# Writing TensorE's order by hand in the attention stage of a hybrid decoder layer

## The chip, the cores and the metric

The kernel runs on one core of a Trainium2 chip. The metric is the device time of one execution in microseconds (us), as the median of several runs. TensorE (PE in the profile) does the matrix products, ScalarE (ACT) the activations and copies, VectorE (DVE) and GpSimd (POOL) elementwise work, and SyncE (SP) issues most of the loads.

## The reference, cut to what matters

One decoder layer on 1024 tokens of width 1024, in float32. The first half mixes tokens: the normalised input is projected once, and the columns of the projection go to two groups of heads. One is attention over a sliding window of 128 with 8 query heads, 2 key-value heads, a learned sink per head and a partial rotation of queries and keys. The other is a gated linear recurrence with 4 heads of 128. Both are normalised, joined and projected. The second half is a dense MLP with squared ReLU.

```python
h = rmsnorm(x, pre_w_mix[l]) * (1.0 + sc1) + sh1
proj = h @ w_in[l]
aq, ak, av, hq, hf, hi, hg = jnp.split(proj, _SPLITS, axis=-1)
aq = partial_rope(aq.reshape(B, T, ATT_Q_HEADS, ATT_HEAD_DIM))
ak = partial_rope(ak.reshape(B, T, ATT_KV_HEADS, ATT_HEAD_DIM))
attn = sliding_window_sink_attention(aq, ak, av, attn_sinks[l])   # softmax over two 128-blocks, with sink
attn = rmsnorm(attn, attn_out_w[l])
...
rec = hgrn2_chunkwise(hq4, 1.0 - f, hv4, jnp.log(f))              # hv4 comes from hi
mix = jnp.concatenate([attn, rec], axis=-1) @ w_out[l]
x = x + g1 * rmsnorm(mix, post_w_mix[l])
```

## The kernel before, in words

Tokens are handled in eight blocks of 128 (`tb` from 0 to 7, `TB` = 8), and the width of 1024 in eight blocks of 128 (`kb`, `KB` = 8). A float32 operand of a projection is split into a high and a low part, and a projection is made of three products a `kb`: high by high, high by low, low by high (`proj3`, line 517). A projection of one token block is thus 24 products into one PSUM bank: of 512 columns for the queries (tile `pq`, weights `wq`) and for the recurrence's values (`pv`, weights `whv`), and of 256 columns for keys and values (`pk`, weights `wkv`).

The kernel is written with a framework that traces instructions, sets the semaphores and gives out the buffers of its pools. A scheduler in it sets the order of each engine's instructions ahead of time, by readiness in its own model and by the place in the text. A small class `Queue` (line 28) stands before each engine. While an engine is pinned (`pin(True, ...)`), each instruction is chained behind the one issued before it, so the engine runs them in the order of the text. Once it is unpinned, instructions are only held behind the last pinned one, and the scheduler orders them. Up to line 689 all compute engines are pinned; line 690 unpins them.

The queries of blocks 0 to 5 and the keys and values of blocks 0 to 3 are projected before that line. What is left for the attention stage is: the keys and values of blocks 4 to 7, the queries of blocks 6 and 7, and the recurrence's values of all eight blocks. They serve as filler between the steps of attention.

The generator `attention(tb)` (line 577) holds one block's attention. By the names of the tiles:

- `pqT`, `pkT`: the queries and keys are transposed on PE and copied (`qT` by ACT, `kT` by DVE).
- `sc`: the scores against this block and the one before, in two halves (`mp`). ACT copies the older block's part into `comb` and DVE copies this block's part under the mask `mle`.
- DVE takes the maximum (`mx`), ACT the exponentials, DVE and POOL divide by the sum.
- `pT`: the weights are transposed on PE; DVE parts them into this block's (`pc`) and the older block's (`pp`).
- `oT`: the output; ACT squares it (`sqa`), DVE multiplies it by `attw` and sums the squares (`sqr`).
- `ssp`: the sums are transposed on PE, DVE reduces them (`ssc`), POOL makes the reciprocal root (`t_att`, `r_att`), DVE puts it on a diagonal (`dg`).
- `rb`: a product spreads it, and DVE multiplies the output by it. The result stays in the tile of the queries.

Before the change the generator has three parts, cut behind the division, behind `dg`, and at the end. The loop at line 723 runs `i` from 0 to 15: at each `i` it takes the parts of the blocks that are due by `att_a` and then one filler, a whole projection of 24 products. With the eighth filler the weights `whv` are loaded and split (`load_split`, line 244: a load by SP, a high part by ACT, a low part by DVE). They take the slots of the pool `g_` that `wq` and others held. At `i` of 12, 13 and 15 a piece of the adaLN modulation begins (`mods`; `modrow` at line 168, `modcols` at line 157): eight loads of 256 KB on SP and the sum `macc` on DVE; for the first two also a broadcast on POOL's queue and a split. PSUM has two banks for projections (`mm_ps`), five for attention (`tp_ps`) and one (`pa`) that `ssp` and `rb` share.

After the stage come the four heads of the recurrence, whose first projection is `phf`, with weights `whf0`.

Of the kernel before, what the change touches and what calls it, by code (L numbers as in the profile page):

```python
# [19 lines left out]
TB = 8  # L20
# [27 lines left out]
def hybrid_layer(ctx: ExitStack, tc: tile.TileContext, I, out, dbg=None):  # L48
# [3 lines left out]
    def pin(on, *engines):  # L52
        for e in engines:
            e.pinned = on
# [478 lines left out]
    cosT = cload("cosT", [P, TB, 16], pool=XA)  # L533
    sinT = cload("sinT", [P, TB, 16], pool=XA)

    def qproj(tb):
        if tb < 6:
            pq = pq0[tb]
        else:
            pq = mm_ps(f"pq{tb}")  # L540
            proj3(pq, htok(tb), wq)
        q = m_(f"q{tb}")
        ACT.activation(q, pq, AF.Copy, scale=0.125)
        qn.append(q)

    def kvproj(tb):
        if tb < 4:
            pk = pk0[tb]
        else:
            pk = mm_ps(f"pk{tb}")  # L550
            proj3(pk[:, :256], htok(tb), wkv)
# [25 lines left out]
    def attention(tb):  # L577
# [8 lines left out]
        kT = XA.tile([P, P], F32, tag="kT", bufs=3, name=f"kT{tb}")  # L586
        DVE.tensor_copy(kT, pkT[:, :P])
        kTs[tb] = kT
        aw = q
        a3 = aw.rearrange("p (m t) -> p m t", m=4)  # L590
        c5 = w_(f"comb{tb}", (P, 2, 2, 2, P))
# [4 lines left out]
        for mp in range(2):  # L596
            scs = [tp_ps(f"sc{tb}_{mp}_{g}").rearrange("p (m j) -> p m j", m=2) for g in range(2)]
            for m in range(2):
                for src in (tb - 1, tb) if tb else (tb,):
                    for g in range(2):  # L600
                        gs = slice(64 * g, 64 * g + 64)
                        js = slice(P, 2 * P) if src == tb else slice(0, P)
                        PE.matmul(scs[g][:, m, js], lhsT=qT[gs, 2 * mp + m, :], rhs=kTs[src][gs, :],
                                  start=True, stop=True)
            for g in range(2):
                sc = scs[g]
                if tb:
                    ACT.activation(c5[:, mp, g], sc[:, :, 0:P], AF.Copy)
                DVE.copy_predicated(c5[:, mp, g], mb, sc[:, :, P:2 * P])
        mx = small.tile([P, 8], F32, tag="mx", name=f"mx{tb}")  # L610
        DVE.tensor_reduce(mx, c, AX.X, ALU.max)
        mx2 = small.tile([P, 8], F32, tag="mx2", name=f"mx2{tb}")
# [57 lines left out]
    def step(tb):  # L670
        if 0 <= tb < TB:
            next(att[tb])

    att = [attention(tb) for tb in range(TB)]
    pq0.append(a_ps("pq4"))
# [16 lines left out]
    def filler(i):  # L692
        if i < 8:
            (kvproj if i % 2 else qproj)(4 + i // 2)
            rope(4 + i // 2, 2 if i % 2 else 8)
        else:
            values(i - 8)


    whv = []  # L700
    hv = []

    def values(tb):
        if not tb:
            for kb in range(KB):
                whv.append(load_split(g_, f"whv{kb}", I["w_hv"][kb]))
        pv = mm_ps(f"pv{tb}")
        proj3(pv, htok(tb), whv)
        v = hv_(f"hv{tb}")
        ACT.activation(v, pv, AF.Copy)  # L710
        hv.append(v)

    a2 = tiny1.tile([P, KB], F32, tag="a2", name="a2")
    sh2 = tiny1.tile([P, KB], F32, tag="sh2", name="sh2")
# [1088 lines left out]
```

## Time and profile before

| what | value |
|---|---|
| median of 3 runs | 1085.75 us (1085.65 to 1085.79) |
| the profiled execution's own time | 1085.71 us |
| its span, first to last instruction | 1083.8 us |
| TensorE's granted clock, mean | 0.998 |
| TensorE busy | 1068.5 us of the span |
| VectorE busy | 806.9 us |
| ScalarE busy | 589.1 us |
| GpSimd busy | 373.8 us |
| DMA traffic | 205.74 MB |

Busy time counts an engine's instructions without what its sequencer does. Matmuls overlap in their pipeline and their ends are modelled, so the spacing of their starts says more than their lengths. A bracket behind a row of a timeline gives the engine's idle time just before that row and what ended it. Nearly all instructions carry line 39, which is the `Queue` class's call, so the rows are told apart by their tiles.

### The profile page before, as it was taken

To read this page: it belongs to the slowest core of one execution; us is meant where nothing else is said; L and a number is where in the kernel's file an instruction comes from. 1 tells how busy PE (TensorE), PEld (TensorE's weight loads), DVE (VectorE), ACT (ScalarE), POOL (GpSimd) and SP (SyncE) were. 2 spreads that over 40 slices of the span, in tenths; PEclk is the share of its full clock that TensorE was granted. 3 is DMA by queue.
4 is the path that set the end of the run, shared out by engine and by line. 5 is a ranking of instruction groups with operands and counts; after the bars stand their busy time and mean duration, and the time that the engine had idled before them with its cause. 6 is when DMAs were issued, how large, how long until landed. Compare 5 with 4: busy or idle time off the path is not lost.

```text
span 1083.8 us, 16059 instructions
## 1 busy us (share of the span) xinstructions
PE 1068.5 (99%) x5449; PEld 872.3 (80%) x5449; DVE 806.9 (74%) x1329; ACT 589.1 (54%) x1215; POOL 373.8 (34%) x497
## 2 busy tenths in 40 slices
PE   8999999999999999999999999999999999999996
PEld 6887676788888888888888888888888888888885
DVE  4877778878765664558777767776767787899886
ACT  4556453546456655576655555555764544456434
POOL 1263211233325653423443434444333333230014
PEclk9999999999999999999999999999999999999999
DMA  9904002444211242323676777767998888998638
GB/s 358 345 21 130 27 1 82 156 148 137 75 59 55 95 173 94 130 89 126 214 250 216 252 233 231 258 219 259 326 355 295 276 292 265 313 325 285 192 95 141
DMA packets 102979, 205.74 MB, mean 190 GB/s; under 512 B 13168, under 2 KB 13936, under 8 KB 102896
## 3 DMA queue, kind: packets, MB, share of 16 engines
q1 hardware_dynamic: 87408, 157.14, 42.7%
q0 software_dynamic: 15200, 47.20, 14.8%
q8 instruction: 43, 0.70, 0.3%
q10 hardware_dynamic: 288, 0.36, 0.1%
q14 instruction: 40, 0.33, 0.1%
HBM read 149.60 MB, written 55.05 MB: 189 GB/s over the span
## 4 chain that ended last, share of the span: by engine, by line
PE 90%; DVE 4%; DMA 3%; ACT 1%; issue 1%; POOL 1%; DVEq 0%; SPq 0%; ACTq 0%; POOLq 0%
PE pda L39 16%; PE pua L39 14%; PE pdc L39 8%; PE po L39 8%; PE puc L39 7%; PE pu L39 4%; PE pdb L39 4%; PE phg L39 4%; PE phq L39 4%; PE pub L39 4%; PE phf L39 3%; PE pv L39 3%; PE pq L39 3%; DMA wa<-wada 1%; PE o L39 1%; DVE macc L39 1%
## 5 line engine op out<-in xcount | busy, mean ns | idle before, releaser
L39 POOL TENSOR_TENSOR b<-b,b 128x512 f32<-128x512 f32 x64 | 90.1, 1407 | 235.8 <-DMA b<-w_dn 235.5
L39 ACT ACTIVATE s<-s 128x512 f32<-128x512 f32 x84 | 52.9, 631 | 32.8 <-DVE s L39 31.5
L39 ACT ACTIVATE dw<-dwr 128x512 fp32r<-128x512 f32 x72 | 45.4, 631 | 41.4 <-DMA dwr<-td 24.7
L39 DVE TENSOR_TENSOR acc<-pda,acc 128x512 f32<-128x512 f32 x68 | 46.5, 684 | 15.0 <-PE pda L39 14.6
L39 DVE TENSOR_TENSOR dw<-dwr,dw 128x512 fp32r<-128x512 f32 x72 | 53.2, 739 | 5.6 <-ACT dw L39 5.6
L39 POOL DMA_DIRECT2D td<-b x64 | 36.3, 567 | 19.0 <-POOL b L39 19.0
L39 ACT ACTIVATE s<-pua 128x512 f32<-128x512 f32 x28 | 16.7, 596 | 40.0 <-PE pua L39 34.5
L39 DVE TENSOR_TENSOR wt<-s,wt 128x512 fp32r<-128x512 f32 x42 | 35.5, 846 | 2.6 <-ACT wt L39 2.5
L39 ACT ACT_TABLE_LOAD x28 | 35.9, 1283 | 1.7 <-PEq L1796 1.2
L39 POOL TENSOR_TENSOR rrf<-ssf,mhalf 128x1 f32<-128x1 f32 x7 | 7.8, 1107 | 83.3 <-DVE ssf L39 83.3
L39 DVE SCALAR_TENSOR_TENSOR macc<-wada,cs,macc 128x512 f32<-128x512 f32 x42 | 33.7, 803 | 2.2 <-DMA wada<-wada 1.7
L39 POOL DMA_DIRECT2D b<-w_dn x64 | 34.4, 540 | 2.5 <-issue 2.5
L39 PE MATMUL pua<-bt_0h,wt 128*128 128x512 f32 x84 | 32.7, 389 | 0.0
L39 PE MATMUL pua<-bt_1h,wt 128*128 128x512 f32 x84 | 32.7, 389 | 0.0
L39 PE MATMUL pua<-bt_2h,wt 128*128 128x512 f32 x84 | 32.7, 389 | 0.0
L39 PE MATMUL pua<-bt_3h,wt 128*128 128x512 f32 x84 | 32.7, 389 | 0.0
L39 DVE TENSOR_TENSOR wt<-a,wt 128x512 fp32r<-128x512 f32 x42 | 31.8, 758 | 0.9 <-ACT wt L39 0.9
L39 POOL TENSOR_TENSOR comb<-comb,rd 128x512 f32<-128x512 f32 x8 | 11.7, 1457 | 59.9 <-DVE rd L39 44.2
L39 ACT ACTIVATE wt<-s 128x512 fp32r<-128x512 f32 x42 | 26.3, 627 | 8.4 <-DVE s L39 8.2
L39 DVE TENSOR_TENSOR acc<-pdc,acc 128x512 f32<-128x512 f32 x36 | 24.6, 684 | 7.2 <-PE pdc L39 7.1
L39 PE MATMUL pdc<-dw,du_3h 128*128 128x512 f32 x96 | 29.6, 389 | 0.0
L39 PE MATMUL pda<-dw,du_7h 128*128 128x512 f32 x96 | 29.6, 389 | 0.0
(768 smaller groups left out, 3748.7 us busy)
## 6 DMA issues: line engine op xcount, KB each, us to landing
dur<-ud SPq DMA_DIRECT2D x112, 256.0 KB, 4.9
wada<-wada SPq DMA_DIRECT2D x64, 256.0 KB, 3.5
b<-w_dn POOLq DMA_DIRECT2D x64, 256.0 KB, 5.5
td<-b POOLq DMA_DIRECT2D x64, 256.0 KB, 3.4
dwr<-td SPq DMA_DIRECT2D x64, 256.0 KB, 4.6
a<-w_u SPq DMA_DIRECT2D x56, 256.0 KB, 4.2
dwr<-w_dn SPq DMA_DIRECT2D x48, 256.0 KB, 4.8
ud<-s SPq DMA_DIRECT2D x42, 256.0 KB, 3.6
```

Source lines behind the costliest of these rows:

```text
L39: ins = op(*args, **kw)
```

## The change

The generator `attention` is cut into seven parts in place of three: behind the copies of `qT` and `kT`, between the halves of the scores, behind the division as before, behind `pc` and `pp`, behind `sqr`, behind `dg` as before, and at the end.

The projections become closures for single products in a list `feed_q`. `feed(us)` takes products from its front until their stated times (0.227 us for 512 columns, 0.12 us for 256) add up to `us`. The last product of a projection also issues its copy and its rotation. PE stays pinned, so that it runs products and steps as written, until the turn t = 6 of the loop; ACT, DVE and POOL are unpinned as before. The loads of `whv` and their splits stand earlier in the text, ahead of the last queries' products. The first two pieces of the modulation begin at t = 6 and 7, the third behind the loop.

```diff
+    feed_q = []
+    def feed(us):
+        while us > 0 and feed_q:
+            fn, w = feed_q.pop(0)
+            fn()
+            us -= w
+    def queue3(pst, lhs, rhs, us, done):
+        n = len(lhs)
+        for k in range(n):
+            for i in range(3):
+                def fn(k=k, i=i):
+                    (ah, al), (bh, bl) = lhs[k], rhs[k]
+                    PE.matmul(pst(), lhsT=al if i == 2 else ah, rhs=bl if i == 1 else bh,
+                              start=(k == 0 and i == 0), stop=(k == n - 1 and i == 2))
+                    if k == n - 1 and i == 2:
+                        done()
+                feed_q.append((fn, us))
...
         kTs[tb] = kT
+        yield
...
                 DVE.copy_predicated(c5[:, mp, g], mb, sc[:, :, P:2 * P])
+            if not mp:
+                yield
...
                 DVE.tensor_tensor(pp[:, mp], pT3, pc[:, mp], ALU.subtract)
+        yield
         o_ps = tp_ps(f"oT{tb}")
...
         DVE.tensor_reduce(sqr, sq.rearrange("p (m t) -> p t m", m=4), AX.X, ALU.add)
+        yield
         ssp = pa.tile([P, 512], F32, tag="aps", name=f"ssp{tb}")
...
-    pin(False, ACT, DVE, POOL, PE)
+    pin(False, ACT, DVE, POOL)
...
+    def values(tb):
+        pv = bank(f"pv{tb}")
+        def done():
+            v = hv_(f"hv{tb}")
+            ACT.activation(v, pv(), AF.Copy)
+            hv.append(v)
+        queue3(pv, htok(tb), whv, 0.227, done)
...
-    att_a = (4, 5, 6, 7, 8, 9, 10, 11)
-    mod_a = (12, 13, 15)
-    for i in range(16):
-        for tb in range(TB):
-            if i in (att_a[tb], att_a[tb] + 2, att_a[tb] + 3):
-                step(tb)
-        filler(i)
-        if i in mod_a:
-            next(mods[mod_a.index(i)])
+    for tb in (4, 5):
+        qproj(tb)
+        rope(tb, 8)
+    for tb in (4, 5):
+        kv_later(tb)
+    for tb in (6, 7):
+        q_later(tb)
+        kv_later(tb)
+    def step(tb):
+        if tb < TB:
+            next(att[tb], None)
+    feed(4.4)
+    step(0)
+    feed(0.9)
+    step(0)
+    step(0)
+    for kb in range(KB):
+        whv.append(load_split(g_, f"whv{kb}", I["w_hv"][kb]))
+    for tb in range(TB):
+        values(tb)
+    feed(4.8)
+    step(1)
+    feed(1.9)
+    step(1)
+    step(1)
+    feed(1.2)
+    step(0)
+    feed(2.6)
+    for t in range(TB):
+        if t > 5:
+            next(mods[t - 6])
+        step(t)
+        step(t + 2)
+        feed(2.6 if t < 6 else 2.8)
+        step(t + 2)
+        step(t)
+        step(t + 2)
+        feed(1.0 if t < 6 else 2.2)
+        if t == 6:
+            pin(False, PE)
+        step(t)
+        step(t + 1)
+        if t < 6:
+            feed(3.3)
+        else:
+            feed(99)
+    next(mods[2])
     gactx.close()
```

`bank(name)` gives a projection its PSUM bank when its first product is issued. `kv_later` and `q_later` are made like `values`, with the copy and the rotation in their last call.

More of the change, by code (lines that the diff above doesn't have):

```diff
@@ L534, in hybrid_layer, with bank, pst @@
     sinT = cload("sinT", [P, TB, 16], pool=XA)
-    def qproj(tb):
[L537 to L541, printed above, removed]
+    feed_q = []
[15 more added lines that the diff above has]
+                feed_q.append((fn, us))
+    def bank(name):
+        got = []
+        def pst():
+            if not got:
+                got.append(mm_ps(name))
+            return got[0]
+        return pst
+    def qproj(tb):
+        pq = pq0[tb]
         q = m_(f"q{tb}")
@@ L546, in kvproj @@
     def kvproj(tb):
[L547 to L551, printed above, removed]
+        pk = pk0[tb]
         kv = XA.tile([P, 256], F32, tag="kv", bufs=8, name=f"kv{tb}")
@@ L668, in attention @@
         yield
-    def step(tb):
-        if 0 <= tb < TB:
-            next(att[tb])
     att = [attention(tb) for tb in range(TB)]
@@ L689, in hybrid_layer, with kv_later, q_later, done @@
         rope(tb, 2, eng)
-    pin(False, ACT, DVE, POOL, PE)
[L692 to L697, printed above, removed]
+    pin(False, ACT, DVE, POOL)
     whv = []
     hv = []
-    def values(tb):
[L704 to L711, printed above, removed]
+    def kv_later(tb):
+        pk = bank(f"pk{tb}")
+        def done():
+            pk0.append(pk())
+            kvproj(tb)
+            rope(tb, 2)
+        queue3(lambda: pk()[:, :256], htok(tb), wkv, 0.12, done)
+    def q_later(tb):
+        pq = bank(f"pq{tb}")
+        def done():
+            pq0.append(pq())
+            qproj(tb)
+            rope(tb, 8)
+        queue3(pq, htok(tb), wq, 0.227, done)
+    def values(tb):
+        pv = bank(f"pv{tb}")
+        def done():
+            v = hv_(f"hv{tb}")
+            ACT.activation(v, pv(), AF.Copy)
+            hv.append(v)
+        queue3(pv, htok(tb), whv, 0.227, done)
     a2 = tiny1.tile([P, KB], F32, tag="a2", name="a2")
@@ L720, in hybrid_layer @@
         mods += [modcols(3, half, m_, sh2), modcols(4, half, m_, sc2)]
-    att_a = (4, 5, 6, 7, 8, 9, 10, 11)
-    mod_a = (12, 13, 15)
-    for i in range(16):
-        for tb in range(TB):
-            if i in (att_a[tb], att_a[tb] + 2, att_a[tb] + 3):
-                step(tb)
-        filler(i)
-        if i in mod_a:
-            next(mods[mod_a.index(i)])
+    for tb in (4, 5):
+        qproj(tb)
+        rope(tb, 8)
+    for tb in (4, 5):
[42 more added lines that the diff above has]
+    next(mods[2])
     gactx.close()
```

## The prediction

> **What bounds the kernel now.** I read the page first (busy shares, then the chain that ended last), then the busy times by windows of 24 us over the attention stage, then TensorE's own timeline from 74 to 192 us, and last the timelines of VectorE (DVE) and GpSimd (POOL) for the same stretch.
>
> ```profile
> PE 1068.5 (99%) x5449; PEld 872.3 (80%) x5449; DVE 806.9 (74%) x1329; ACT 589.1 (54%) x1215; POOL 373.8 (34%) x497
> ...
> PE 90%; DVE 4%; DMA 3%; ACT 1%; issue 1%; POOL 1%; DVEq 0%; SPq 0%; ACTq 0%; POOLq 0%
> ```
>
> TensorE (PE) is busy throughout and carries 90% of the chain: a microsecond of PE time lost in the stage is a microsecond of the kernel, and so is one saved. The change adds and removes no matmul, so all it can win is time in which PE waits, or issues more slowly than it could.
>
> ```profile
> 122.00:146.00 24.00, 23.98 (x158) 16.99 (x156) 17.23 (x42) 12.27 (x48) 3.46 (x6) 1.00 0.00 1
> ...
> 170.00:194.00 24.00, 22.57 (x101) 16.16 (x100) 21.54 (x37) 7.10 (x12) 4.27 (x6) 1.00 0.43 134
> ```
>
> The columns are length, then busy time of PE, weight load, DVE, ACT and POOL, the granted clock, and DMA. In the middle of the stage PE has no gap and the clock is full; at its end DVE is the fuller engine (21.54 of 24 us). One period of the middle, from PE's timeline (start, length, instructions):
>
> ```profile
> 130.67 1.09 PE L39 MATMUL oT<-pp,kv 128*64 128x512 f32 x4
> ...
> 132.55 0.66 PE L39 MATMUL pqT<-c_tab,q 128*128 128x128 f32 x4
> 133.04 0.27 PE L39 MATMUL pkT<-c_tab,kv 128*128 128x128 f32 x1
> 133.07 0.48 PE L39 MATMUL pv<-whv4h,hhi 128*128 128x512 f32 x1
> ...
> 133.95 0.71 PE L39 MATMUL sc<-kT,qT 64*128 64x128 f32 x8
> 134.59 0.51 PE L39 MATMUL pv<-whv5h,hhi 128*128 128x512 f32 x1
> 135.11 0.33 PE L39 MATMUL ssp<-c_tab,sqr 128*128 128x128 f32 x1
> 135.19 0.47 PE L39 MATMUL pv<-whv5l,hhi 128*128 128x512 f32 x1
> 135.60 1.61 PE L39 MATMUL sc<-kT,qT 64*128 64x128 f32 x24
> 137.13 0.49 PE L39 MATMUL rb<-dg,ones 128*128 128x128 f32 x2
> 137.46 1.04 PE L39 MATMUL pT<-c_tab,comb 128*128 128x128 f32 x8
> 138.25 0.49 PE L39 MATMUL pv<-whv5h,hlo 128*128 128x512 f32 x1
> ...
> 143.25 1.08 PE L39 MATMUL oT<-pp,kv 128*64 128x512 f32 x4
> ```
>
> Start to start, three products take 133.95-133.07 = 0.88 us and 21 products 143.25-138.25 = 5.00. So a product costs (5.00-0.88)/18 = 0.229 us, and each unbroken group of products 0.19 us more, for entering and leaving the attention's fp32 work. The two groups of one product cost 0.52 and 0.41, or 0.29 and 0.18 over the product. The period is 12.58 us with 3+1+1+21 = 26 products: 5.95 us for products, 6.63 for everything else. Ahead of and behind this steady part PE does wait (the bracket is the idle time and what ended it):
>
> ```profile
> 94.87 0.94 PE L39 MATMUL sc<-kT,qT 64*128 64x128 f32 x12
> ...
> 97.39 0.49 PE L39 MATMUL pq<-wq7h,hlo 128*128 128x512 f32 x1
> 98.24 0.49 PE L39 MATMUL rb<-dg,ones 128*128 128x128 f32 x2 [0.36 <-DVE dg L39]
> ...
> 104.60 1.09 PE L39 MATMUL oT<-pp,kv 128*64 128x512 f32 x4 [0.29 <-DVE pp L39]
> ...
> 109.62 0.33 PE L39 MATMUL ssp<-c_tab,sqr 128*128 128x128 f32 x1 [0.37 <-DVE sqr L39]
> ...
> 112.04 0.49 PE L39 MATMUL rb<-dg,ones 128*128 128x128 f32 x2 [0.55 <-DVE dg L39]
> ...
> 173.01 1.06 PE L39 MATMUL pT<-c_tab,comb 128*128 128x128 f32 x8 [0.42 <-DVE comb L39]
> ...
> 174.59 0.30 PE L39 MATMUL ssp<-c_tab,sqr 128*128 128x128 f32 x1 [0.28 <-DVE sqr L39]
> ...
> 177.02 0.49 PE L39 MATMUL rb<-dg,ones 128*128 128x128 f32 x2 [0.31 <-DVE dg L39]
> ...
> 191.38 0.49 PE L39 MATMUL rb<-dg,ones 128*128 128x128 f32 x2 [0.43 <-DVE dg L39]
> ```
>
> Every wait is for DVE: 0.36+0.29+0.37+0.55 = 1.57 us early, 0.42+0.28+0.31+0.43 = 1.44 late.
>
> **The change, part by part.** *Order.* Names: step 1 is pqT/pkT, 2 and 3 the two halves of sc, 4 pT, 5 oT, 6 ssp, 7 rb. A feed of 2.6 us pops 12 value products (12 x 0.227 is the first sum past 2.6), 1.0 pops 5 and 3.3 pops 15. One turn of the new loop is oT(t), pqT(t+2), 12 products, sc half, ssp(t), sc half, 5 products, rb(t), pT(t+1), 15 products. Attention steps without sc: oT 132.55-130.67 = 1.88, pqT and pkT 133.07-132.55 = 0.52, rb 0.33, pT 0.79, together 3.52. The sc block with ssp inside it isn't split by products any more: from below 0.64+0.08+1.53 = 2.25 (the three pieces of the period above without the products between them), from above 97.39-94.87 = 2.52 (ssp in mid-block). I take 2.40, between two near rows. Three groups cost 3 x 0.19 = 0.57. That is 6.49 us beside the products against 6.63: 0.14 saved a turn, five turns (t=1 to 5), **-0.7**. The turn has 32 products, so it lasts 6.49+7.33 = 13.8 us instead of 12.58; that costs nothing by itself, the queue just empties earlier: 27 value products are left when t=6 begins and 4 after its two feeds.
>
> *Early and late waits.* If the hand-set groups cover them, 1.57 and 1.44 go. Group counts ahead of the third pT are 9 before and 10 after (+0.2), behind the last but one oT 6 and 5 (-0.2). Sum with everything covered: -0.7-1.57-1.44 = **-3.7**.
>
> *What is late next.* PE's order is now fixed, so a step that isn't ready stops all products queued behind it, and each cover has to be checked against DVE's chain:
>
> ```profile
> 134.00 1.05 DVE L39 TENSOR_REDUCE sqr<-sqa 128x128 f32<-128x512 f32 x1
> ...
> 135.47 0.29 DVE L39 TENSOR_REDUCE ssc<-ssp 128x1 f32<-128x128 f32 x1 [0.23 <-PE ssp L39]
> 136.71 0.29 DVE L39 TENSOR_SCALAR dg<-c_tab,r_att 128x128 f32<-128x128 f32 x1 [0.94 <-POOL r_att L39]
> 136.98 1.45 DVE L39 COPY_PREDICATED comb<-c_mle,sc 128x256 f32<-128x256 int32 x4
> 138.32 0.68 DVE L39 TENSOR_TENSOR q<-q,rb 128x512 f32<-128x512 f32 x1
> ...
> 141.47 1.28 DVE L39 TENSOR_TENSOR pp<-pT,pc 128x512 f32<-128x512 f32 x2
> ```
>
> - sc waits for qT: 0.88 us of products sufficed; now 12 x 0.229+0.19 = 2.94. Hidden.
> - ssp waits for sqr: oT's end 132.55 to 135.05 is 2.5 us; now 0.52+2.94+1.0 (an sc half) = 4.5. Hidden, with 2.0 to spare for DVE work put ahead of it.
> - rb waits for dg: ssp's start to dg's end is 137.00-135.11 = 1.89 us, and 112.04-109.62 = 2.42 where PE waited. The cover is ssp 0.26, sc half 1.0, five products 5 x 0.229+0.19 = 1.34: 2.6 us. But the predicated copies of the first sc half (1.45/4 = 0.36 each) are now ready before dg, where they came behind it. One ahead of it makes 2.25 to 2.78.
> - oT waits for pp: from the multiply by rb at 138.32 to the end of pp at 142.75 is 4.43 us of solid DVE work. The multiply can't start before rb has run (0.33), so 4.76 from rb's start; the cover is 0.33+0.79+15 x 0.229+0.19 = 4.75. Nothing is left over.
>
> The last two lose between 0 and 0.3 us each a turn. I take 0.15 a turn in all, since each sum just meets its cover: five turns, **+0.75**.
>
> In turns 0 and 1 DVE also subtracts the eight value weights (whv, low halves). They go into the slots that the query weights hold, so they follow the products of q7 here as before; only their place in the text moves ahead. One such subtraction takes 0.68 us (the 110.29 row below). The old order shows the stretch: rb to oT lasted 104.60-98.24 = 6.36 us and held 1.45 of copies, which now come mostly before rb, and one subtraction. 6.36-1.45 = 4.91 is 0.16 over the cover with one of them in it, 0.84 with two, and nothing with none. I take two, for the loads of the later ones land through this stretch: **+0.8**.
>
> POOL's part of rb's chain shows two lengths:
>
> ```profile
> 110.29 0.68 DVE L39 TENSOR_TENSOR whv7l<-whv7r,whv7h 128x512 fp32r<-128x512 f32 x1
> ...
> 110.45 0.56 POOL L39 TENSOR_SCALAR t_att<-ssc 128x1 f32<-128x1 f32 x1 [0.85 <-DVE ssc L39]
> ...
> 135.85 0.19 POOL L39 TENSOR_SCALAR t_att<-ssc 128x1 f32<-128x1 f32 x1 [1.48 <-DVE ssc L39]
> ```
>
> At 135.85 DVE stood still; at 110.45 it was in a subtraction. The difference, 0.37 us, is what separates the 1.89 chain from most of the 2.42 one. The Trainium skill ("SBUF — State Buffer", section "SBUF: two separate sides") says that VectorE and GpSimd share one port pair as an exclusive lock, taken also by a VectorE instruction with two SBUF inputs, and the other engine is then blocked for the whole instruction. The two rows agree. By that rule a copy that reads scores from PSUM wouldn't slow POOL and five turns lose about nothing at rb; if it does, each loses 0.2, 1.0 in all.
>
> *The moved loads.* The modulation's pieces: each issues eight 256 KB loads on SP, one row broadcast on POOL's queue for the first two, and nine DVE instructions. The first moves from behind step 6 of block 6 to ahead of its oT, the third from ahead of the last values to behind the loop. SP has nothing else then that PE waits for, so the loads cost nothing; the DVE work is the rival below. Unpinning PE at t=6 lets the first head's products fill behind the last value.
>
> Sum: -3.7+0.75+0.8 = -2.15, and the product that stands alone at 97.39 (0.85 us for what costs 0.42 in a group, 0.07 of it beyond its bracket), the one at 173.8 and the stops inside the third block's scores, which no bracket shows in full, about -0.2: **-2.35**. The profiled execution took 1085.71 us (1083.8 span and 1.9 around it), the median 1085.75. Forecast: 1083.4.
>
> **The rivals.** *No new waits.* The scheduler that still orders DVE may put pc and pp ahead of the max-reduce, which frees 1.1 us before oT; then -3.7-0.2 = -3.9: 1081.8. Against it: DVE in turn 0 and 1.
>
> *Waits that only move.* The Trainium skill ("TensorE: Matmul & The Clock Gate", Part 2) says that matmuls stay in program order and only weight loads are pulled ahead. Row 98.24 shows it as a mechanism of this kernel: PE stood 0.36 us before rb with products behind it. If each of the 3.0 us of waits comes back at another step (oT instead of rb, early), only -0.7 stays: 1085.0.
>
> *DVE bounds the end (slower).*
>
> ```profile
> 170.66 0.75 DVE L39 SCALAR_TENSOR_TENSOR macc<-wada,cs,macc 128x512 f32<-128x512 f32 x1
> ...
> 181.94 0.68 DVE L39 TENSOR_TENSOR whf0l<-whf0r,whf0h 128x512 fp32r<-128x512 f32 x1
> ```
>
> Behind the last but one oT, DVE owes block 6 about 2.6 us (multiply, sqr 1.05, ssc, dg, multiply), block 7 four passes of 0.64, the modulation 8 x 0.75 = 6.0 and whf0l 2 x 0.68: 12.5 us. PE brings 27 products (6.2), three groups and two short steps: 7.9. Then oT(7) comes 4.6 us late, and the head's products can't fill because whf0l stands in the same queue; ssp and rb of block 7 wait again (0.28+0.43 above). -2.35+5.3 = +2.9: 1088.6. It decides once more than 2.35 us of that is on the path. Against it: the modulation's loads land long before, so DVE can do this work in its pauses of turn 5 (17.23 of 24 us busy), and the old end hid the same work.
>
> That the change doesn't take effect is excluded: PE's instructions are chained in the written order.
>
> **How the numbers follow.** A measurement tells 0.2% (2.2 us) from no change. Forecast 0.42 (own range 1082.4 to 1084.4; 0.34 of it below 1083.6), no new waits 0.16, waits that move 0.26, DVE at the end 0.16 (0.15 above 1087.9). So faster 0.50, same 0.35, slower 0.15. The range leaves out most of the slower case and the far end of the best one: 1081.5 to 1087.0.
>
> **What would show it.** Right: a turn near 13.8 us with three product groups; oT(1) at a wait of about 0.8; brackets of 0 to 0.3 before rb and oT in turns 2 to 5; the head's first product between the last value and oT(7). Wrong: turns of 14.1 or more, a PE wait over 1 us after 172 us, or head products that start later than at 187.68 less the gain so far.

## The result, and the profile after

The changed kernel takes 1093.43 us (median of 6 runs, 1092.55 to 1094.86), the kernel before beside it 1085.77 us (6 runs, 1085.59 to 1086.22). The ratio is 1.0071, with a 95% interval of 1.0058 to 1.0084: slower by 7.7 us, where 1083.4 us was forecast and 1087.0 was the range's upper end. The profiled execution of the changed kernel is the fastest of its runs, 1092.55 us with a span of 1090.6.

The page, against the one of before (busy shares; engines' shares of the chain that ended last):

```profile
PE 1068.6 (98%) x5449; PEld 874.1 (80%) x5449; DVE 804.9 (74%) x1329; ACT 590.8 (54%) x1215; POOL 371.1 (34%) x497
...
PE 87%; DVE 5%; DMA 4%; ACT 1%; issue 1%; POOL 1%; SPq 0%; DVEq 0%; ACTq 0%; POOLq 0%
```

PE's work is the same (1068.6 us against 1068.5), but its part of the chain fell from 90% to 87%: the added time is time in which PE stands or runs slowly. The busy times by windows say where (columns as before):

```profile
122.00:146.00 24.00, 23.92 (x163) 17.70 (x160) 15.83 (x35) 10.36 (x37) 4.39 (x6) 1.00 0.00 1
...
170.00:194.00 24.00, 18.70 (x100) 12.77 (x100) 21.51 (x40) 8.12 (x28) 3.80 (x5) 1.00 0.30 88
```

The middle is as full as it was. At the end PE has 18.70 of 24 us busy where it had 22.57, and DVE is as full as before. One turn of the middle on PE's timeline of the changed kernel:

```profile
135.53 1.08 PE L39 MATMUL oT<-pp,kv 128*64 128x512 f32 x4
...
137.40 0.66 PE L39 MATMUL pqT<-c_tab,q 128*128 128x128 f32 x4
...
137.92 0.48 PE L39 MATMUL pv<-whv7h,hhi 128*128 128x512 f32 x1
...
140.83 1.16 PE L39 MATMUL sc<-kT,qT 64*128 64x128 f32 x16
141.93 0.33 PE L39 MATMUL ssp<-c_tab,sqr 128*128 128x128 f32 x1
142.18 1.16 PE L39 MATMUL sc<-kT,qT 64*128 64x128 f32 x16
143.28 0.50 PE L39 MATMUL pv<-whv3h,hhi 128*128 128x512 f32 x1
...
144.54 0.38 PE L39 MATMUL rb<-dg,ones 128*128 128x128 f32 x2
144.76 1.04 PE L39 MATMUL pT<-c_tab,comb 128*128 128x128 f32 x8
145.55 0.48 PE L39 MATMUL pv<-whv4h,hlo 128*128 128x512 f32 x1
...
149.31 1.08 PE L39 MATMUL oT<-pp,kv 128*64 128x512 f32 x4
```

The turn lasts 149.31-135.53 = 13.78 us, with three groups of products and no bracket. PE's waits in the changed kernel (who waited for whom: total, times, longest; from 84 to 125 us, then from 168 to 205; between the two there is none):

```profile
PE sc L39 <- ACT qT L39: 2.6, 1, 2.6
PE oT L39 <- DVE pp L39: 0.8, 1, 0.8
...
PE rb L39 <- DVE dg L39: 2.6, 3, 1.8
PE oT L39 <- ACT comb L39: 1.6, 1, 1.6
PE phf L39 <- ACT whf0h L39: 1.2, 1, 1.2
PE oT L39 <- DVE pp L39: 0.3, 1, 0.3
```

Early 3.4 us where there were 1.57, at the end 5.7 where there were 1.44. And the first of them costs more than its length. The windows around it, first of the changed kernel, then of the one before (the third column from the end is the granted clock):

```profile
94.50:97.00 2.50, 0.17 (x1) 0.00 (x0) 1.47 (x5) 1.52 (x5) 1.04 (x1) 1.00 0.61 178
97.00:101.00 4.00, 3.70 (x31) 3.26 (x33) 3.76 (x8) 1.42 (x4) 0.13 (x1) 0.57 0.28 96
```

```profile
94.50:97.00 2.50, 2.49 (x31) 1.82 (x32) 2.50 (x5) 0.91 (x3) 0.92 (x2) 1.00 0.00 0
97.00:101.00 4.00, 3.64 (x35) 3.21 (x32) 3.25 (x9) 2.44 (x6) 2.68 (x6) 1.00 0.57 139
```

PE stood from 94.7 to 97.3, and then its clock was 0.57 on average over 4 us. In finer windows it is 0.5 for 3.4 us. The scores' first half, 16 matmuls, takes 99.31-97.30 = 2.01 us there, where 1.10 is usual (141.93-140.83):

```profile
97.30 2.08 PE L39 MATMUL sc<-kT,qT 64*128 64x128 f32 x16 [2.63 <-ACT qT L39]
99.31 0.47 PE L39 MATMUL ssp<-c_tab,sqr 128*128 128x128 f32 x1
99.71 1.63 PE L39 MATMUL sc<-kT,qT 64*128 64x128 f32 x16
```

So (1-0.57) x 4.0 = 1.7 us are lost on top of the 2.63. In the kernel before, the granted clock is 1.00 in all windows of the stage.

To add this up I use a ledger: the start-to-start time of PE's instructions from 55 us on, less 0.2265 us a product of 512 columns (0.120 for 256) and less what each attention step takes undisturbed. What is left is waiting, changing between kinds of work, and a lowered clock. Blocks count from 0, so `rb1` is block 1's. Up to the second rb (`rb1`) it is 4.9 us before and 7.7 after; from there to `rb4` 3.6 and 3.2; from there to the last, `rb7`, 4.3 and 8.8. The differences are **+2.8, -0.4 and +4.5**, 6.9 in all. PE's starts behind the stage are 6.8 us later down to the end of the kernel, so nothing else matters in this execution.

### The profile page after: what moved, and what is told of

Read it like the earlier page. It is cut to its first block, busy times and chain, and to the rows that moved or that the text cites. A ratio compares the mean times of both kernels' runs of the same rounds, so it can differ in the third digit from the quotient of the medians.

```text
span 1090.6 us, 16057 instructions
## 1 busy us (share of the span) xinstructions
PE 1068.6 (98%) x5449; PEld 874.1 (80%) x5449; DVE 804.9 (74%) x1329; ACT 590.8 (54%) x1215; POOL 371.1 (34%) x497
## 4 chain that ended last, share of the span: by engine, by line
PE 87%; DVE 5%; DMA 4%; ACT 1%; issue 1%; POOL 1%; SPq 0%; DVEq 0%; ACTq 0%; POOLq 0%
PE pda L39 16%; PE pua L39 14%; PE pdc L39 8%; PE po L39 8%; PE puc L39 7%; PE phg L39 4%; PE pu L39 4%; PE pdb L39 4%; PE phq L39 3%; PE pub L39 3%; PE phf L39 3%; PE pv L39 2%; PE pq L39 2%; DMA wa<-wada 2%; PE o L39 1%; PE sc L39 1%
## 5 line engine op out<-in xcount | busy, mean ns | idle before, releaser
L39 POOL TENSOR_TENSOR b<-b,b 128x512 f32<-128x512 f32 x64 | 87.6, 1368 | 211.2 <-DMA b<-w_dn 210.9
L39 DVE TENSOR_TENSOR wt<-a,wt 128x512 fp32r<-128x512 f32 x42 | 34.5, 821 | 0.9 <-ACT wt L39 0.9
L39 ACT ACTIVATE comb<-comb,nm 128x128 f32<-128x128 f32 x64 | 24.8, 388 | 18.5 <-DVE sd L39 16.0
L39 DVE TENSOR_TENSOR s<-puc,s 128x512 f32<-128x512 f32 x14 | 9.7, 690 | 30.0 <-issue 27.5
L39 PE MATMUL pda<-dw,du_6h 128*128 128x512 f32 x96 | 29.5, 389 | 0.0
```

What stands on the lines that cost most here:

```text
L39: ins = op(*args, **kw)
```

## The experiments

Theory A: the work of ACT and DVE that was moved ahead in the text (splits of the value weights, sums of the modulation) holds up attention's chain. Theory B: PE's fixed order is what costs. Theory C, formed after the first four runs: the hand order spends 32 products a turn where the old one spent 26, and the end runs bare. Theory D, formed last: the clock. All results in one table; the ledger's parts are to rb1, rb1 to rb4, and rb4 to rb7; "half clock" is the time that the lowered clock took in the stage and in the first head behind it, half the length of each fall. It is an upper bound, for in some falls PE stood for a part of it. Ledger and half clock are those of one profiled execution each, the medians are not: that of `mods_later` was the slowest of its four (1096.03 us).

| kernel | median, us (range) | ratio, 95% | ledger, us | half clock, us |
|---|---|---|---|---|
| before (beside `after`) | 1085.77 (1085.59-1086.22) | | 4.9 / 3.6 / 4.3 | 0 |
| after | 1093.43 (1092.55-1094.86) | 1.0058-1.0084 | 7.7 / 3.2 / 8.8 | 1.7 |
| whv_later | 1091.29 (1090.85-1091.75) | 1.0032-1.0065 | 6.2 / 3.1 / 8.9 | 1.7 |
| mods_later | 1094.04 (1093.71-1096.03) | 1.0064-1.0094 | 10.6 / 3.2 / 9.2 | 6.8 |
| both_later | 1093.46 (1091.05-1093.63) | 1.0050-1.0080 | 6.3 / 3.2 / 10.4 | 3.4 |
| order_free | 1089.10 (1088.29-1092.11) | 1.0022-1.0049 | 5.7 / 2.7 / 7.4 | 0 |
| free_both | 1091.51 (1090.76-1091.89) | 1.0037-1.0067 | 5.0 / 2.8 / 9.9 | 3.4 |
| save_products | 1088.42 (1086.28-1089.74) | 1.0011-1.0035 | 9.6 / 3.4 / 3.9 | 3.4 |
| mods_behind | 1096.34 (1095.71-1098.45) | 1.0087-1.0121 | 6.1 / 3.2 / 4.1 | 3.4 |
| all_three | 1097.05 (1096.24-1097.88) | 1.0089-1.0119 | 8.3 / 3.2 / 2.6 | 5.1 |
| save_alone | 1092.25 (1091.66-1093.45) | 1.0047-1.0074 | 9.2 / 3.3 / 7.0 | 3.4 |
| keep_cover | 1088.22 (1087.44-1089.06) | 1.0012-1.0030 | 6.1 / 4.5 / 4.2 | 0 |
| keep_free | 1087.00 (1085.53-1090.08) | 1.0004-1.0021 | 5.3 / 3.7 / 4.3 | 0 |
| old_whv_early | 1092.42 (1089.96-1094.03) | 1.0044-1.0069 | 7.6 / 3.5 / 4.8 | 1.7 |
| old_mods_early | 1086.74 (1086.35-1087.80) | 0.9999-1.0017 | 4.9 / 3.6 / 5.3 | 0 |
| warm_after | 1092.43 (1091.51-1094.14) | 1.0046-1.0070 | 7.0 / 3.2 / 8.8 | 0 |
| warm_save | 1090.45 (1090.07-1090.94) | 1.0025-1.0049 | 7.3 / 3.3 / 7.0 | 0 |

In `mods_behind` the whole 3.4 us of half clock and in `all_three` 3.4 of the 5.1 lie behind the stage. The unread products of the two `warm_` kernels count as lost time in the ledger.

**1. The moved places put back, in the hand order.** For `whv_later` the loads and splits of `whv` go behind rb and pT of the loop's first turn; for `mods_later` each piece of the modulation goes behind ssp; `both_later` does both.

```diff
     step(0)
-    for kb in range(KB):
-        whv.append(load_split(g_, f"whv{kb}", I["w_hv"][kb]))
...
-        if t > 5:
-            next(mods[t - 6])
...
         step(t)
+        if t > 5:
+            next(mods[t - 6])
         step(t + 2)
...
         step(t + 1)
+        if not t:
+            for kb in range(KB):
+                whv.append(load_split(g_, f"whv{kb}", I["w_hv"][kb]))
```

Expected of `whv_later`: 

> The changed kernel with the loads and splits of the value weights written behind pT(1), just ahead of the first value product, and not ahead of the last queries' products. Theory A: ACT no longer has copies that wait for loads ahead of qT(2), so the wait of 2.6 us at the scores goes; some of it may come back at the first value products, if the splits are late: 1090 to 1092 us. Theory B: the splits still have to be done in this stretch and the fixed order stops somewhere in it: 1092.5 or more.

Expected of `mods_later`: 

> The changed kernel with the modulation's pieces begun behind ssp of blocks 6 and 7, where the old text had them, and not ahead of oT. Theory A (the loss is side work that moved ahead of attention on DVE and ACT): the waits of TensorE before rb(5) (1.8 us), oT(6) (1.6) and most of that before oT(7) go, the wait at the scores of block 2 (2.6) stays: 1088 to 1090 us. Theory B (the fixed order of TensorE is the cause, and any DVE work turns into such waits): the modulation only waits somewhere else, 1091.5 or more.

Expected of `both_later`: 

> The changed kernel with both moves undone (modulation and value weights), TensorE's order still fixed. Theory A: the two gains add, 1084.5 to 1087 us, near the kernel before. Theory B: 1090 or more.

The wait for qT is gone from `whv_later`, but 1.8 us before oT(1) and 1.2 before the scores came in its place, and 2.1 us were won (the intervals overlap). `mods_later` was no faster than the change. Its waits before rb5 and oT(6) went, but the first product of the next head (`phf`) then waited 1.2 us and oT(7) 2.2. Its early wait for qT was 3.56 us, though nothing ahead of it had been edited: ACT stood 2.27 us for the load of `whv4r`, where in the changed kernel's trace it stood 0.98 us for `whv5r`. So that wait varies with the landing of the loads. With both moves undone nothing is won at all. The end's waits of `both_later`:

```profile
PE oT L39 <- DVE pp L39: 2.2, 1, 2.2
PE phf L39 <- ACT whf0h L39: 1.2, 1, 1.2
...
```

The waits before rb5 and oT(6) went and appeared before oT(7), where 1.20 and 2.23 us of idle time stand close together and the clock falls to half for 6.8 us. Theory A alone falls: in neither place did the end have enough to cover the work. Behind rb6 PE has 4 value products left in all these kernels, where it had 36 before the change.

**2. PE's order left to the scheduler, with the change's text.** `order_free` unpins PE at the stage's start; `free_both` does so with the text of `both_later`.

```diff
-    pin(False, ACT, DVE, POOL)
+    pin(False, ACT, DVE, POOL, PE)
...
-        if t == 6:
-            pin(False, PE)
```

Expected of `order_free`: 

> The changed kernel with TensorE unpinned for the whole stage, so that the scheduler orders its products, and the text otherwise as changed (modulation and value weights early). Theory A: DVE's and ACT's queues are as full as before, so most of the loss stays: 1089 to 1093 us. Theory B: the scheduler fills the waits with products: 1085 to 1087 us.

Expected of `free_both`: 

> As both_later with TensorE unpinned for the whole stage: the seven parts and single products remain, the order is the scheduler's. Theory A: the text's order of side work was all that cost it in order_free, so 1085 to 1087 us. If the finer cut or the feeds' place in the text cost by themselves, 1088 or more, as order_free (1089.1).

Free order wins 4.3 us of the 7.7, clear of the intervals; 3.2 stay. In the profiled executions 1.7 of the 4.3 is the clock, but other executions of `order_free` had mean clocks down to 0.993. `free_both` was to come near the kernel before and is slower than `order_free`. Both spend the products as the hand order does (4 value products behind rb6) and meet the same bare end: 7.4 us in the ledger's last part of `order_free`, and 7.3 of `free_both` without the 2.6 us that PE lost there by half clock while it worked. So theory B has a part, more than half with the change's text, 2.0 us with that of `both_later` (overlapping intervals), and not the whole.

**3. Fewer products a turn.** `save_products` is `both_later` with 8 products in place of 12 behind pqT in turns 1 to 5. `save_alone` does only that to the changed kernel. `keep_cover` is `both_later` with 12 in turns 0 and 1 and 6 in turns 2 to 5. `keep_free` is `keep_cover` with PE left to the scheduler.

```diff
-        feed(2.6 if t < 6 else 2.8)
+        feed((1.8 if t else 2.6) if t < 6 else 2.8)            # save_products, save_alone
+        feed(2.6 if t < 2 else 1.3 if t < 6 else 2.8)          # keep_cover, keep_free
```

Expected of `save_products`: 

> As both_later (modulation and value weights where the old text had them, TensorE's order fixed), and turns 1 to 5 pop 8 products behind pqT in place of 12, so 28 a turn in place of 32 and 20 more products are left for the end. Theory C (the loss at the end is that the hand order has spent its products by then, 27 left where the old order had 88 from pT(6) on, so nothing covers DVE's chain): the waits before oT(7) and rb(7) of 3.8 and 3.2 us shrink by the 4.5 us that 20 products last: 1088 to 1090 us. Theory A (it is only where the modulation's DVE work stands, and that is already undone here): no change, 1092.5 to 1094.

Expected of `save_alone`: 

> The change as it is, but with 8 products instead of 12 behind the transposition of queries in turns 1 to 5 (28 a turn instead of 32, so 20 products more are left for the last two turns); nothing else is moved. Theory C (the hand order spends the products too fast and the last turns run bare): the 4.5 us that are lost between the fifth rb and the last go, the 2.8 us lost in the first turn stay: about 1089 us. Theory A (the place of the value weights' and the modulation's work in the text makes the loss, the number of products matters little): over 1091.5 us, the multiply-adds of the modulation still hold up oT(6) by over 1 us.

Expected of `keep_cover`: 

> Value weights and modulation moved back as in the run with both moved, 12 products behind the transposition of queries in turns 0 and 1, but only 6 in turns 2 to 5 (26 a turn, as the old order used). Theory C with the early cover kept: PE's loss to the first rb is 6.3 us as with both moved back (9.6 us when turn 1 too was cut to 8 products), from the first rb to the last about 7.3 us as in the run that saved products: 0.8 us above the kernel before in all, 1086.0 to 1087.5 us. Theory B (an order that PE may not leave costs some 3 us of its own, whatever the number of products): 1088 us or more.

Expected of `keep_free`: 

> The text of the run that kept cover (value weights and modulation back, 26 products in turns 2 to 5), with TensorE's order left to the scheduler over the whole stage. Theory B (the fixed order itself costs the 2.3 us by which that run is still above the kernel before): 1085.5 to 1086.8 us. Rival (the order of the text is left a worse one, whoever sorts it, or the moved steps of ScalarE and VectorE are): 1087.5 to 1089 us.

`save_products` came where theory C had put it, 5.0 us under `both_later`, clear of the intervals. PE's waits at its end, and those between 80 and 130 us:

```profile
PE rb L39 <- DVE dg L39: 1.1, 2, 0.6
...
PE sc L39 <- DVE kT L39: 2.1, 1, 2.1
PE oT L39 <- DVE pp L39: 1.5, 1, 1.5
```

The end is as short as the old one (3.9 us in the ledger). But eight products no longer cover kT's copy, which stands behind the subtractions on DVE in turn 1: 2.1 us, and half clock behind them. `keep_cover` leaves those twelve alone, has full clock throughout the stage, and is the best with a fixed order: 1088.22, a little over what theory C said and just within B's. What is left above the kernel before is early (6.1 against 4.9) and in the middle (4.5 against 3.6), where six products behind pqT fall 0.1 to 0.2 us a turn short of kT's copy, about half of that loss. `save_alone`, expected at about 1089, gave 1092.25, with overlapping intervals: twenty more products help little while the modulation's sums still stand ahead of oT(6), where PE waits 1.6 us as in the changed kernel. Without the half clock during which PE worked (3.0 us of `both_later`) the ledger's last part is 8.8 as changed, 7.4 with the sums moved (7.5 in `mods_later`), 7.0 with products kept, 3.9 with both, and 4.3 before. Neither cause is enough alone, and removing either alone gives less than half. `keep_free` lies between what its two theories said (1087.00); it takes off 1.2 us with overlapping intervals, so with this text no more than that can be said of the fixed order's own cost.

**4. The modulation moved out of the stage.** `mods_behind` is `both_later` with all three pieces behind the loop; `all_three` also has 28 products a turn, and the loads of `whv` ahead of the first turn's twelve products.

```diff
-        if t > 5:
-            next(mods[t - 6])
...
-    next(mods[2])
+    for mod in mods[:3]:
+        next(mod)
```

Expected of `mods_behind`: 

> As both_later, and all three pieces of the modulation begin behind the loop, so that DVE has none of their 27 instructions ahead of rb(7). Theory A: the waits at the end go with them, 1088 to 1090 us. Theory C: DVE's own chain pT to oT still stands bare of products, so about half the waits stay: 1090 to 1092 us.

Expected of `all_three`: 

> Fixed order; value weights written behind pqT of block 2 (so that qT of block 2 is ahead of them on ACT, and earlier than in whv_later), modulation behind the loop, 28 products a turn. Theory A and C together: early waits near the old ones, none above 1 us at the end: 1084.5 to 1087 us. If a fixed order loses by itself: 1088 or more.

The expectations failed by 4.3 us (`mods_behind`, against theory C's upper end) and by 10 (`all_three`, where only the rival, 1088 or more, was met), though the end of the stage did as they said: 4.1 and 2.6 us in the ledger. The early part of `all_three` did not (8.3 us): oT(1) waited 3.8 us there. Most of the loss came next, in the heads of the recurrence. A row of PE's waits, two of DVE's timeline and two windows of `mods_behind`:

```profile
PE phq L39 <- DVE sg L39: 7.8, 1, 7.8
```

```profile
217.52 0.75 DVE L39 SCALAR_TENSOR_TENSOR macc<-wada,cs,macc 128x512 f32<-128x512 f32 x1 [1.00 <-DMA wada<-wada]
218.19 0.74 DVE L39 SCALAR_TENSOR_TENSOR sg<-phg,c_hgw,sg 128x512 f32<-128x512 f32 x1
```

```profile
211.20:215.50 4.30, 0.01 (x1) 0.00 (x0) 3.69 (x6) 1.02 (x2) 0.00 (x0) 1.00 0.60 198
215.50:222.50 7.00, 3.52 (x8) 2.81 (x9) 5.83 (x11) 4.73 (x7) 0.00 (x0) 0.51 0.48 149
```

The head's `sg`, whose reading frees a PSUM bank for `phq`, stands on DVE behind sums of the modulation and splits of the next head's weights; one of the sums waited 1.00 us for its load. That the bank is what `phq` waits for is read from the tiles and was not tested. PE stands 7.8 us. The clock is halved from 215.6, in the middle of that wait, to 222.5, so PE's first 3.5 us of work behind it run at half speed. The old order had spread these sums one by one between attention's steps.

**5. The moved places alone, in the old order.** `old_whv_early` and `old_mods_early` are the kernel before with only the text's place changed.

```diff
     for i in range(16):
+        if i == 5:                                             # old_whv_early
+            for kb in range(KB):
+                whv.append(load_split(g_, f"whv{kb}", I["w_hv"][kb]))
+        if i in (12, 13):                                      # old_mods_early
+            next(mods[i - 12])
```

The lines that stood at the eighth filler, or behind fillers 12, 13 and 15, go; the third piece stands behind the loop.

Expected of `old_whv_early`: 

> The kernel before, with its own order, and the loads and splits of the value weights issued earlier in the text, ahead of filler step 5 (they stood at step 8). Theory A: the rounding copies on ScalarE and the subtractions on VectorE come between the first softmax and the transposed queries of block 2, which cost 2.6 us in the changed kernel: 1087 to 1089 us. Theory B (it costs only where PE may not take other products while it waits): less than 1 us lost, 1085 to 1086.8 us.

Expected of `old_mods_early`: 

> The kernel before, with its own order, and the three pieces of the modulation begun earlier in the text: ahead of filler steps 12 and 13 (they stood behind 12 and 13) and behind the loop (it stood behind 15). Theory A: the multiply-adds start on VectorE some microseconds earlier and hold up oT of blocks 6 and 7 as in the changed kernel: 1087.5 to 1090 us. Theory C: with 88 products left at that point the cover is there, and less than 1 us is lost: 1085.5 to 1087 us.

Moving the value weights alone costs 6.5 us, far over what theory A had put on it. Of the 5.3 us by which its profiled span is longer, the ledger has 3.1 in the stage; behind it, PE waits 1.3 us for ACT at one `phg` (0.3 before), and the rest is lost among the first head's products. Moving the modulation alone costs 0.9: with products in hand it is nearly covered, as theory C said. ACT's timeline of the changed kernel, of the one before, and of `old_whv_early`:

```profile
93.64 0.63 ACT L39 ACTIVATE whv4h<-whv4r 128x512 fp32r<-128x512 f32 x1
...
95.64 0.63 ACT L39 ACTIVATE whv5h<-whv5r 128x512 fp32r<-128x512 f32 x1 [0.98 <-DMA whv5r<-w_hv]
96.18 0.58 ACT L39 ACTIVATE sqa<-oT 128x512 f32<-128x512 f32 x1
96.66 0.59 ACT L39 ACTIVATE qT<-pqT 128x512 f32<-128x512 f32 x1
```

```profile
93.40 0.57 ACT L39 ACTIVATE qT<-pqT 128x512 f32<-128x512 f32 x1
93.87 0.62 ACT L39 ACTIVATE whv2h<-whv2r 128x512 fp32r<-128x512 f32 x1
```

```profile
94.21 0.63 ACT L39 ACTIVATE whv3h<-whv3r 128x512 fp32r<-128x512 f32 x1 [0.95 <-PE pq L39]
...
97.42 0.58 ACT L39 ACTIVATE qT<-pqT 128x512 f32<-128x512 f32 x1
```

Before, block 2's qT runs first and `whv2h` behind it. Once the splits stand earlier in the text, those up to `whv5h` come between the exponentials of block 1. A load holds them (0.98 us in the changed kernel), or PE's work on the queries does (0.95), and qT is 3.3 us later in the one and 4.0 in the other. In `old_whv_early` PE took 31 products between pkT and the scores, where it took 15 before, and waited 0.5 us for qT. The products were then missing later: 31 in place of 36 behind rb6. PE waited 1.5 us for `sqr` soon after, and the clock fell all the same: 0.57 from 102.5 to 106.5.

**6. The idle time filled, the wait kept.** `warm_after` is the changed kernel, `warm_save` is `save_alone`, each with 9 products that nobody reads ahead of block 2's scores.

```diff
+            if tb == 2 and not mp:
+                for _ in range(9):
+                    PE.matmul(sps[0], lhsT=htok(2)[0][0], rhs=whv[0][0], start=True, stop=True)
```

Expected of `warm_after`: 

> The change as it is, plus 9 products that nobody reads, issued into the scores' own bank ahead of the scores of block 2, where TensorE stood idle for 2.6 us and the granted clock then fell to 0.5 until 101 us. They fill some 2.0 us of the idle time and delay nothing; the wait for the transposed queries stays as long as it was. Theory D (an idle time of 2 us and more costs not its own length alone: the clock is then halved for 3.4 us, which loses 1.7 us, at times 3.4): the clock stays 1.00 to 110 us, 1090 to 1091.8 us, and the runs scatter less. Rival (the clock's fall is no cost of its own, the chain behind the wait sets the time): 1092.5 to 1094 us.

Expected of `warm_save`: 

> The run that saved products alone (8 instead of 12 behind the transposition of queries in turns 1 to 5), plus the same 9 unread products ahead of the scores of block 2. There the idle time was 2.76 us and the clock stood at 0.5 for two spells of 3.4 us, 98.5 to 106. Theory D: the clock stays 1.00, 3.4 us are won: 1088.5 to 1089.8 us, which is where theory C alone had put the run without them. Rival: 1091.5 to 1093 us as without them.

The same window of `save_alone` and of `warm_save`:

```profile
98.50:106.00 7.50, 6.75 (x38) 6.06 (x37) 6.07 (x13) 2.43 (x6) 2.25 (x6) 0.54 0.31 85
```

```profile
98.50:106.00 7.50, 6.44 (x56) 6.03 (x57) 7.20 (x18) 2.33 (x9) 2.26 (x6) 1.00 0.47 123
```

56 instructions of PE in place of 38 in the same 7.5 us. `warm_save` is 1.8 us faster than `save_alone`, in median and in the profiled execution alike; the ranges of the two lie apart, the intervals of the ratios just touch. That is short of the 3.4 expected, and PE's timeline of `warm_save` shows why:

```profile
94.67 2.20 PE L39 MATMUL sc<-whv0h,hhi 128*128 128x512 f32 x9
96.81 1.16 PE L39 MATMUL sc<-kT,qT 64*128 64x128 f32 x16
99.56 0.33 PE L39 MATMUL ssp<-c_tab,sqr 128*128 128x128 f32 x1 [1.59 <-DVE sqr L39]
```

The scores run at full clock, and then PE waits 1.59 us for `sqr`, which the slow scores had hidden. `warm_after` won 1.0 us in the profiled execution and in the median (the ledger: 7.7 to 7.0 us at rb1). That lies between what theory D and its rival said, with overlapping intervals, and the runs scatter no less (2.6 us against 2.3). So theory D holds in direction, in the trace and in `warm_save`, and its price is what is left after the next wait.

No version here beats the kernel before. In the middle, from rb1 to rb4, the fixed orders of 28 and 32 products a turn gain 0.2 to 0.5 us in the ledger, the free orders of 32 gain 0.8 to 0.9, and `keep_cover` with 26 loses 0.9. So the gain there is not the hand order's own, and it lies under what a measurement of the whole tells.

## Why the prediction was wrong, step by step

Two terms failed: the move of the weight splits, whose half on ACT was put at nothing, and the faster spending of the products together with the moved sums, put at nothing as well. Point by point:

- *The order* was sized rightly. A turn was to last 13.8 us and lasts 13.78; three groups a turn; the saving of 0.14 us a turn makes 0.42 for three turns, and the ledger has 0.4 from rb1 to rb4.
- *sc waits for qT: "Hidden"* failed in turn 0. The cover of 2.94 us was counted from pqT, as if ACT copied at once; ACT's queue was not looked at. The wait was 2.63 us.
- *"They follow the products of q7 here as before; only their place in the text moves ahead"* is the step behind it. Six of the eight splits came ahead of block 2's qT in place of two. The prediction priced DVE's half of the split alone, and ACT's half at nothing. The 0.8 us that it put before oT(1) came out (0.77), but by luck: it took two subtractions to stand in that stretch, and there was one (`whv7l`). With the splits put back (`whv_later`) the wait for qT was gone; in the old order (`old_whv_early`) the move alone costs 6.5 us.
- *What a wait costs* was taken as its length. The lowered clock added 1.7 us in the profiled execution of the changed kernel, and up to 5.8 in that of another (`mods_later`, counting only time in which PE worked).
- *rb* did not wait in the middle, and oT waited little: 15 products from 145.55 to 149.31 take 3.76 us against 15 x 0.229+0.19 = 3.63, so 0.13, where 0.15 a turn was put for both. Rows of DVE and of POOL in a turn of the middle show why rb had no loss:

```profile
142.50 0.77 DVE L39 COPY_PREDICATED comb<-c_mle,sc 128x256 f32<-128x256 int32 x2
143.53 0.28 DVE L39 TENSOR_SCALAR dg<-c_tab,r_att 128x128 f32<-128x128 f32 x1 [0.27 <-POOL r_att L39]
```

```profile
142.67 0.19 POOL L39 TENSOR_SCALAR t_att<-ssc 128x1 f32<-128x1 f32 x1 [3.84 <-DVE ssc L39]
```

  Two copies did come ahead of `dg`, and POOL's step beside them kept its short length, 0.19 us. That is the case for which the prediction had cited the Trainium skill ("SBUF — State Buffer", "SBUF: two separate sides"): by that rule a copy that reads scores from PSUM does not block POOL, and the trace agrees. In turn 5 the same step took 0.62 us at 172.45, beside a sum of the modulation on DVE.
- *"That costs nothing by itself, the queue just empties earlier"* failed: it is theory C. The 27 value products left at t = 6 and the 4 behind its two feeds were counted rightly, but not what they had to cover. The late 1.44 us of waits were to go and became 5.7, with a share of the next point's in it.
- *The moved loads: "the loads cost nothing; the DVE work is the rival"*. The rival came in kind and in size, not in place. Its working gave +5.3 for the end against the forecast, and the end came out 5.9 over it (-1.44 forecast, +4.5 measured). But it had oT(7) 4.6 us late, and that waited 0.3; the waits were before rb(5), oT(6) and `phf`, so the close size is in part luck. It had a chance of 0.16 because DVE "can do this work in its pauses of turn 5". The rows of DVE's timeline after show what became of that:

```profile
165.42 1.26 DVE L39 TENSOR_SCALAR macc<-wada,cs 128x512 f32<-128x512 f32 x1
...
168.40 3.10 DVE L39 SCALAR_TENSOR_TENSOR macc<-wada,cs,macc 128x512 f32<-128x512 f32 x4
171.42 0.77 DVE L39 COPY_PREDICATED comb<-c_mle,sc 128x256 f32<-128x256 int32 x2
172.08 0.28 DVE L39 TENSOR_REDUCE ssc<-ssp 128x1 f32<-128x128 f32 x1
...
188.39 1.53 DVE L39 SCALAR_TENSOR_TENSOR macc<-wada,cs,macc 128x512 f32<-128x512 f32 x2
189.84 0.68 DVE L39 TENSOR_TENSOR q<-q,rb 128x512 f32<-128x512 f32 x1
```

  The sums did move into turn 5, four of them in a row, but ahead of the copies and of `ssc` on which rb(5) hangs, and PE waited 1.8 us there. Two more stand ahead of the multiply by rb in the last turn. That multiply's operand was there when rb(6) ended, at 189.0, and it started at 189.84, behind the second sum, as the order set ahead of time has it. A pause of DVE is thus only of use to work that stands behind what the pause waits for. Its free microseconds (17 of 24 busy) were read as room anywhere.

In sum, -2.35 us were forecast and +6.84 came in the profiled execution, 9.2 apart: 3.8 early (-1.0 against +2.8), 5.9 at the end, and 0.5 the other way in the middle (+0.05 for its five turns, against -0.4 for the three from rb1 to rb4). Of the signs that the prediction had named, the turn near 13.8 us and the wait of 0.8 before oT(1) came. So did those of its being wrong: waits of 1.8, 1.6 and 1.2 us after 172 us, and the head's first product at 192.03.

What stays open: `keep_free` is 1.1 us above the kernel before. Its profiled execution (1088.58 us, above its median) is 1.2 us behind by 220 us and loses 1.4 more near the end of the kernel, far from any edit. What the fixed order costs by itself stays open too: 4.3 us with the change's text, 1.2 with that of `keep_cover`. That the scatter of the changed kernel's runs (2.3 us, against 0.6 before) is the clock as well fits their mean clocks (0.993 to 0.997, against 0.998 in the profiled execution before), but only one of them has a trace.

## What to carry to other kernels

When steps are moved in a text from which a scheduler or a hand order is made, follow every engine that a moved step uses, ACT's copy as well as DVE's, and ask which instruction of the chain stands behind it in that queue and what it may have to wait for itself. Filler is a stock: count what a turn spends against what the bare end needs, for a middle that spends faster gains nothing while PE is busy anyway. And when one move fails, try the causes in pairs: here two single repairs gave little, and both together gave 5 us.

## What the runs showed of the hardware

A wait of PE can cost more than its length. Set against the clock in the traces of all runs, every idle spell of 2.07 us or more came with a clock of 0.5. The spells are 2.07, 2.63, 2.76, 3.56 and 3.78 us, 1.20 with 2.2 close behind it, and 7.31 and 7.77 behind the stage. The fall began within the spell or at most 1.6 us behind it; in three of the longest (3.56, 7.31 and 7.77) it began 2.2, 4.7 and 4.4 us after PE had stopped. Spells of 1.2 to 1.9 us mostly left it at 1.00 (`after`: 1.81, 1.63 and 1.20 near the end; `order_free`: 1.61 and 1.90), but it fell behind 1.82 us in `whv_later` and, among several shorter waits, behind 1.54 in `old_whv_early`. Half clock lasted 3.4 or 6.8 us at a time, once 10.2 (`mods_later`); 3.4 us of it cost 1.7 us of work, and less where PE stood anyway. The Trainium skill ("TensorE: Matmul & The Clock Gate", "Part 1: The HAM clock gate") tells of a free-running window of about 3.4 us by which the clock is halved or restored; the lengths here agree with it. The same page's rule of thumb in "HAM oscillation — how this bites in real kernels", that idle gaps over some 3.4 us are to be avoided, is too mild for this case: 1.8 to 2.8 us were enough. In the kernel before no wait of the stage is over 0.6 us, so its trace could not show this.
